# A two-layer attention encoder: value products over four query tiles, half of them between a tile's two score components

## The chip, the cores and the metric

The kernel runs on one core of a Trainium2 chip. The metric is the device time of one execution in microseconds (us); several executions are timed and their median is given. TensorE (PE) multiplies matrices; VectorE (DVE), ScalarE (ACT) and GpSimd (POOL) work element by element; SyncE (SP) issues the DMAs.

## The reference

Input is `x` (1024 rows of 1024, float32). Two layers follow, each a normalised, shifted and scaled copy of `x` (scale, shift and output gate come from a conditioning vector `c`), an attention branch times a SiLU gate, an output projection and a gated residual add; a final norm closes.

```
layer 0 (8 heads): q, k: two components of 64 per head, rotated by position; v: 128 per head
    p = softmax(q1 k1 / 8) - lam * softmax(q2 k2 / 8)      # 1024 x 1024 per head
    o = p @ v;  o = rmsnorm(o) * silu(z);  x = x + gate * (o @ w_out)
layer 1 (8 heads): low-rank q (384) and kv (256), per head k_nope, q_nope of 128, a shared rotated k_pe of 64
    p = softmax((q_nope k_nope + q_pe k_pe) / sqrt(192))
    o = p @ v;  o = o * silu(z);  x = x + gate * (o @ w_out)
```

## The kernel before

Every large product is made of three matmuls (`mm3`, lines 184 to 186): both operands are split into a high and a low part, and high by high, low by high and high by low are summed in PSUM.

**Attention.** A head has two halves of four query tiles of 128 rows; a tile is the unit of the loops in `attn0` and `attn1`. In layer 0, `q_tile` makes the scores of a tile's component 0, then those of component 1, each in a PSUM tile `s` of two banks (two such tiles are in use, so each component comes back to its own one tile later). A component's scores are four matmuls of 512 columns: two halves of the keys by two stacked parts of q. VectorE takes the row maximum (line 399), ScalarE the exponential (line 401; component 1 in place), and VectorE combines both (line 781) into `e`. In layer 1, `scores1` has ten matmuls for a tile (line 1611), one maximum and one exponential.

**Turning and values.** A finished tile `e` is turned by `transpose_p` in two groups of keys, `kh` 0 and 1: four transposes into the one PSUM bank `tr` (line 382), a copy by ScalarE into `pth`, the high part (line 384), and a subtraction by VectorE into `ptl`, the low part (line 385). `pv` multiplies the turned probabilities with the value tiles `vt`: 12 matmuls for each `kh`, in which a value block of 128 x 128 is stationary and the columns of `pth` or `ptl` move. Before, `alloc_pt` gives one set of buffers to two query tiles (256 columns), with six buffers under one tag, and `pv` runs over each pair, into the left or right half of the bank `pv`, which is closed after the second pair (`close`: `head_out` and `subln` in layer 0, line 1629 and `finish` in layer 1).

**The order around a tile.** `Tail` keeps what is left to do for the two tiles before. While tile n is made, group 1 of tile n-2 is turned, and its values taken if it ends a pair; group 0 of tile n-1 is turned. In layer 0 the order is: scores 0, `fill(0)`, group 1 of n-2, `fill(1)`, scores 1, `fill(2)`, group 0 of n-1, `fill(3)`, values `kh` 0, `fill(4)`, values `kh` 1, `fill(5)`. In layer 1 group 1 of n-2 stands inside the scores (`SPL1`), and then `fill(0)`, group 0 of n-1, `fill(1)`, values, `fill(2)`, values, `fill(3)`.

**Fills.** `fill(i)` takes steps of a stream (`Stream.step`): the projections of later heads (k, q and gate z in layer 0; k, q and every second head the rotary q in layer 1). A step is one block of 128 of the contraction for a half of the rows, three matmuls of 512 columns into a bank `acc`. In layer 0 a strip has 16 steps, the stream 22 strips (352 steps). The tuples `FILL0` (heads 0 to 6), `FILL7` (head 7, its first four tiles, after which the rest is run off) and `FILL1` give the steps for each place of each tile, and `Z_PRE` those ahead of the first head. In layer 1, heads need 16 or 10 steps by turns (`steps1`), `FILL1` has 12 for every head, and what lacks is run at the head's end. A strip's weights are split by ScalarE and GpSimd (lines 229, 230) while the strip before it runs.

**Deferred work.** The rotary part of k and q is queued in `side`; each step and each tile takes one entry (`tick`). `ROT` and `DEF` say after how many entries the swapped half is multiplied and the result stored in the stacked operands.

**Start of layer 1.** `v1_tile` makes the eight value tiles of layer 1's second half of heads; `store_v` splits each into `v_hl` and stores it to DRAM (`vS`, line 364), from which `load_v` fetches a head's value tiles (line 373). The `v_hl` of these eight use the tag of the turned probabilities, six buffers.

Instructions are dispatched to each engine in an order that a planner makes from the program, so neighbours in the program can be interleaved on TensorE; an engine then runs its queue in order.

Of the kernel before, what the change touches and what calls it, by code (L numbers as in the profile page):

```python
# [12 lines left out]
F32R = mybir.dt.float32r  # L13
# [8 lines left out]
P = 128  # L22
D = 1024
T = 1024
NT = T // P
KT = D // P
HF = 512
# [7 lines left out]
for _n, _c in _W:  # L35
    VEC[_n] = (NVEC, _c)
    NVEC += _c
DEF = 7
ROT = 3
DEF1 = 0  # L40
FILL0 = ((1, 2, 1, 1, 1, 0), (1, 1, 1, 1, 1, 1)) * 3 + ((1, 2, 1, 1, 1, 0), (1, 1, 1, 1, 1, 0))
FILL1 = ((1, 0, 1, 0), (0, 1, 0, 0)) * 4
SPL1 = 2
Z_PRE = 16
V_LATE = 6
MODS = (2, 2, 2, 2, 3, 2, 0, 0)
V1_AT = (3, 2)
# [7 lines left out]
OP1 = (12, 4)  # L55
LAST = [(((0, 1, 2, 3), 0, HF),), (((0, 1), 0, HF), ((2,), 0, HF), ((3,), 0, 256), ((3,), 256, HF))]
Z_LAST = 4
FILL7 = ((0, 1, 1, 1, 1, 0),) * 4
G_WAIT = 3
G1_AT = 7  # L60
VB = (2, 3)
# [24 lines left out]
def trunk(ctx: ExitStack, tc: tile.TileContext, A, out):  # L86
    nc = tc.nc
# [95 lines left out]
    def mm3(psum, ah, al, bh, bl, first, last):  # L183
        PE.matmul(psum, ah, bh, start=first, stop=False)  # L184
        PE.matmul(psum, ah, bl, start=False, stop=False)  # L185
        PE.matmul(psum, al, bh, start=False, stop=last)  # L186
# [94 lines left out]
    class Side:  # L281


        def __init__(self):
            self.q = []
# [70 lines left out]
            SP.dma_start(f32v(t[64:128, 0, :]), f32v(t[0:64, 0, :]))  # L356
            SP.dma_start(f32v(t[0:64, 1, :]), f32v(t[64:128, 1, :]))

    def store_v(l, sp, acc, tt, fh, tag="vst", bufs=None):
        v = sp.tile([P, 2, HF], F32R, name="v_hl", tag=tag, bufs=bufs or VB[l])  # L360
        S.copy(v[:, 0, :], acc)
        V.tensor_sub(v[:, 1, :], acc, f32v(v[:, 0, :]))  # L362
        th, tl = tt // 4, tt % 4
        SP.dma_start(
            vS[l][fh][:, th, :, :, tl, :].rearrange("h p l d -> p l h d"),
            f32v(v).rearrange("p l (h d) -> p l h d", h=4),
        )
# [19 lines left out]
    def pv(o_, vt, pth, ptl, kh):  # L387
        for j in range(4):
            mm3(o_, vt[kh][:, 0, j, :], vt[kh][:, 1, j, :], pth[kh][:, j, :], ptl[kh][:, j, :], kh + j == 0, kh * 4 + j == NT - 1)

    def alloc_pt(ap_):
        pth = [ap_.tile([P, 4, 2 * P], F32R, name="pth", tag="pt", bufs=6) for _ in range(2)]
        ptl = [ap_.tile([P, 4, 2 * P], F32R, name="ptl", tag="pt", bufs=6) for _ in range(2)]
        return pth, ptl

    def softmax_part(ap_, s_ps, zs, bufs=3):

# [471 lines left out]
    class Tail:  # L869


        def __init__(self, qp, t, e, zz, c):
            self.qp, self.t, self.e, self.zz, self.c = qp, t, e, zz, c
            self.mate = tails[1]

        def turn(self, kh):
            if kh == 0:
                self.pt = alloc_pt(self.c["pool"]) if self.t == 0 else self.mate.pt
                self.mate = None
            transpose_p(self.e, *self.pt, self.t, kh)  # L880

        def pv(self, kh):
            c, qp = self.c, self.qp
            if self.t == 0:
                return
            if kh == 0:
                if qp == 0:
                    c["vt"] = load_v(c["pool"], c["l"], c["h"])
                if qp % 2 == 0:
                    c["o_"] = bank("pv", "pv")  # L890
                    c["open"](qp // 2)
            cs = slice((qp % 2) * 256, (qp % 2) * 256 + 256)
            pv(c["o_"][:, cs], c["vt"], *self.pt, kh)
            if kh == 1 and qp % 2 == 1:
                c["close"](qp // 2, c["o_"], self.zz)

    tails, hooks = [None, None], []

    def run_tails(fill):

        prev, last = tails
        prev.turn(1)
        fill(0)
        last.turn(0)
        prev.pv(0)
        prev.pv(1)
        fill(1)
        last.turn(1)
        fill(2)
        last.pv(0)  # L910
        last.pv(1)
        tails[:] = [None, None]

    def after_scores(fill, n):

        prev, last = tails
        if last:
            last.turn(0)
        fill(n)
        if prev:  # L920
            prev.pv(0)
        fill(n + 1)
        new = hooks[:]
        if prev:
            prev.pv(1)
        fill(n + 2)
        for f in new:
            hooks.remove(f)
            f()

    def attn0(h, fills, extra=None, late=None):

        def close(half, o_, zz):
            if late and half == 1:
                ctx_["late"] = late(o_, zz)
                return
            o = a0b.tile([P, HF], F32, name="o", tag="o", bufs=2)
            sq = a0b.tile([P, HF], F32, name="osq", tag="osq", bufs=4)
            head_out(o_, o, sq)
            subln(o, sq, zz, half, h, None)  # L940

        ctx_ = dict(pool=a0b, l=0, h=h, open=lambda half: None, close=close)
        for qp in range(4):
            half = qp // 2
            if qp % 2 == 0:
                zz = first.pop(0) if first else sm.tile([P, 4], F32, name="zz")
            for t in range(2):
                fl = fills(qp * 2 + t)

                def fill(i):  # L950
                    if fl[i]:
                        stream0.step(fl[i])

                def mid(c):
                    if c == 0:
                        fill(0)
                        if tails[0]:
                            tails[0].turn(1)
                        fill(1)

                if first:
                    e0 = first.pop()
                else:
                    e0 = q_tile(h, half, (qp * 2 + t) % 4, zz, a0b, mid)
                    fill(2)
                    after_scores(fill, 3)
                side.tick()
                tails[:] = [tails[1], Tail(qp, t, e0, zz, ctx_)]
                if extra:
                    extra(qp * 2 + t)  # L970
        if late:
            run_tails(lambda i: extra(8 + i))
            while hooks:
                hooks.pop(0)()
            return ctx_["late"]
# [492 lines left out]
            G.tensor_sub(l_, raw, f32v(h_))  # L1468
            wk[k][fh] = (h_, l_)

    def v1_tile(tt, fh, sp, *buf):
# [5 lines left out]
        store_v(1, sp, acc, tt, fh, *buf)  # L1477

    CK, CQ = [[None, None] for _ in range(2)], [[None, None] for _ in range(3)]

# [61 lines left out]
    gate1 = gate_steps()  # L1542
# [75 lines left out]
    def attn1(h, fills, extra=None, late=None):  # L1618

        def open_(half):  # L1620
            ctx_["gz"] = wst.tile([P, HF], F32, name="gz1", tag="gz", bufs=3)
            SP.dma_start(ctx_["gz"], zS[h, half])

        def close(half, o_, zz):
            if late and half == 1:
                ctx_["late"] = late(o_, zz, ctx_["gz"])
                return
            o = ap2.tile([P, HF], F32, name="o1", tag="o", bufs=2)
            V.scalar_tensor_tensor(out=o, in0=o_, scalar=0.5, in1=ctx_["gz"], op0=ALU.mult, op1=ALU.mult)
            V.reciprocal(zz, zz)  # L1630
            finish(o, zz, 1, h, half, None, ap2, None)

        ctx_ = dict(pool=ap, l=1, h=h, open=open_, close=close)
        for qp in range(4):
            half = qp // 2
            if qp % 2 == 0:
                zz = first1.pop(0) if first1 else sm.tile([P, 4], F32, name="zz1")
            for t in range(2):
                ti = (qp * 2 + t) % 4
                fl = fills(qp * 2 + t)  # L1640

# [10 lines left out]
                tails[:] = [tails[1], Tail(qp, t, e, zz, ctx_)]  # L1652
                if extra:
                    extra(qp * 2 + t)
        if late:
            run_tails(lambda i: extra(8 + i))
            while hooks:
                hooks.pop(0)()
            return ctx_["late"]

    stream1.step(6)
    v1_left = list(range(NT))
    for n, steps in zip(V1_AT, (steps1[0] - 6, 0)):
        for tt in v1_left[:n]:
            v1_tile(tt, 1, ap, "pt", 6)
        del v1_left[:n]
        stream1.step(steps)
    side.flush()
# [1 line left out]
    zz0 = sm.tile([P, 4], F32, name="zz1")  # L1670
    first1 += [zz0, scores1(0, 0, 0, zz0)]
    for tt in v1_left:
        v1_tile(tt, 1, ap, "pt", 6)
    stv.close()
    ap2 = pool(st5, "attn1b")
    for h in range(NH - 1):
        attn1(h, lambda i: FILL1[i], lambda i: next(gate1, None))
        while late_q:
            late_q.pop(0)()
        stream1.step(sum(steps1[: h + 2]) - stream1.count)  # L1680
# [162 lines left out]
```

## Time and profile before

| | us |
|---|---|
| median of 3 runs | 1441.8 |
| lowest and highest | 1441.35, 1442.82 |
| the profiled execution | 1438.65 |
| its span, first to last instruction | 1436.9 |

Layer 0's attention lies between about 165 and 690 us of the span, layer 1's between about 975 and 1347. How a line of groups reads: line, engine, operation, output and inputs by name, shape, count, then busy time and mean duration of one, then the idle time of that engine just ahead of them and what ended it. A timeline row has start, duration, engine, line, operation, operands, shape and count of merged neighbours.

### The profile page before, as it was taken

How to read it: one execution, taken by the hardware profiler on the slowest of the kernel's cores; microseconds unless marked ns; L12 is line 12 of the kernel's file. 1: busy time of each engine (PE TensorE's matmuls, PEld its weight loads, DVE VectorE, ACT ScalarE, POOL GpSimd, SP SyncE). 2: the span in 40 equal slices, each digit the busy share in tenths (PEclk: the TensorE clock that was granted, in tenths of full speed). 3: DMA queues.
4: the chain of work that ended last, by engine and by line, in shares of the span. 5: the costliest groups of instructions: out<-in, count | busy, mean ns of one | idle time of the engine just before them, and what ended most of it. 6: DMA issues, size and time to landing. Idle time of an engine off the chain costs nothing. (4 is left out here: it accounts for less than half of the span.)

```text
span 1436.9 us, 20644 instructions
## 1 busy us (share of the span) xinstructions
PE 1388.8 (97%) x7388; PEld 1158.8 (81%) x7388; DVE 917.5 (64%) x1372; ACT 728.7 (51%) x1287; POOL 610.6 (42%) x483
## 2 busy tenths in 40 slices
PE   5999999999999999998999999999999999999997
PEld 4778788888888888887787877887888888888886
DVE  6656877767777767677435985545666555555355
ACT  5622375666565656566343452335455554545342
POOL 4416164656464646464461343532141331412572
PEclk9999999999999999999999999999999999999999
DMA  8787723333332333237653145398343432336563
GB/s 326 238 254 237 255 70 93 84 104 81 96 101 84 96 89 91 86 96 248 236 183 125 38 132 184 122 305 236 133 130 111 130 101 77 104 96 217 185 237 136
DMA packets 135527, 213.70 MB, mean 149 GB/s; under 512 B 19072, under 2 KB 56064, under 8 KB 135424
## 3 DMA queue, kind: packets, MB, share of 16 engines
q1 hardware_dynamic: 135424, 212.38, 47.1%
q8 instruction: 58, 0.95, 0.3%
q14 instruction: 45, 0.37, 0.1%
HBM read 137.92 MB, written 50.80 MB: 131 GB/s over the span
## 5 line engine op out<-in xcount | busy, mean ns | idle before, releaser
L384 ACT CAST pth<-tr 128x512 fp32r<-128x512 f32 x256 | 150.6, 588 | 284.2 <-PE tr L382 281.9
L399 DVE TENSOR_REDUCE nm<-s 128x1 f32<-128x1024 f32 x192 | 234.1, 1219 | 77.2 <-PE s L773 65.7
L385 DVE TENSOR_TENSOR ptl<-tr,pth 128x512 fp32r<-128x512 f32 x256 | 176.2, 688 | 139.4 <-ACT pth L384 138.9
L230 POOL TENSOR_TENSOR wl<-wraw,wh 128x512 fp32r<-128x512 f32 (+2 forms) x79 | 103.6, 1314 | 205.6 <-ACT wh L229 183.4
L401 ACT ACTIVATE e<-s,nm 128x1024 f32<-128x1024 f32 x128 | 143.7, 1123 | 29.8 <-DVE nm L399 29.2
L382 PE MATMUL tr<-ident,e 128*128 128x128 f32 x1024 | 155.1, 274 | 2.3 <-DVE ptl L385 2.0
L382 PEld LDWEIGHTS tr<-ident,e 128*128 128x128 f32 x1024 | 121.2, 140 | 43.6 <-DVE ptl L385 19.2
L184 PE MATMUL acc<-h0h,wh 128*128 128x512 f32 x360 | 150.1, 417 | 1.9 <-DVE v_hl L362 1.8
L184 PE MATMUL pv<-pth,vt 128*128 128x256 f32 x512 | 147.1, 287 | 0.0
L185 PE MATMUL pv<-ptl,vt 128*128 128x256 f32 x512 | 145.8, 285 | 0.0
L186 PE MATMUL pv<-pth,vt 128*128 128x256 f32 x512 | 144.7, 283 | 0.0
L186 PE MATMUL acc<-h0h,wl 128*128 128x512 f32 x360 | 143.1, 398 | 0.5 <-POOL wl L230 0.5
L185 PE MATMUL acc<-h0l,wh 128*128 128x512 f32 x360 | 142.0, 394 | 0.0
L1013 POOL TENSOR_TENSOR wol<-wor,woh 128x512 fp32r<-128x512 f32 x64 | 85.0, 1351 | 84.7 <-ACT woh L1012 77.2
L185 PEld LDWEIGHTS pv<-ptl,vt 128*128 128x128 f32 x512 | 97.6, 191 | 2.9
L184 PEld LDWEIGHTS pv<-pth,vt 128*128 128x128 f32 x512 | 97.4, 190 | 2.9 <-ACT pth L384 0.2
L186 PEld LDWEIGHTS pv<-pth,vt 128*128 128x128 f32 x512 | 97.6, 191 | 0.1
L326 POOL TENSOR_TENSOR rp_r<-rp_raw,cosT 128x512 f32<-128x512 f32 x38 | 49.8, 1311 | 91.0 <-ACT rp_raw L321 50.8
L331 POOL TENSOR_TENSOR rp_sw<-rp_sw,sinT 128x512 f32<-128x512 f32 x42 | 55.4, 1318 | 74.1 <-DMA rp_sw<-rp_raw 73.9
L773 PE MATMUL s<-ks,qa 128*128 128x512 f32 x256 | 82.6, 404 | 2.8 <-DVE e L781 2.6
L781 DVE SCALAR_TENSOR_TENSOR e<-s,z,e 128x1024 f32<-128x1024 f32 x64 | 82.1, 1283 | 2.1
L773 PE MATMUL s<-ks,qb 128*128 128x512 f32 x256 | 81.1, 395 | 0.0
(590 smaller groups left out, 3335.4 us busy)
## 6 DMA issues: line engine op xcount, KB each, us to landing
ada<-in_ada_ss SPq DMA_DIRECT2D x32, 512.0 KB, 6.0
wraw<-in_w_s SPq DMA_DIRECT2D x64, 256.0 KB, 2.9
vS<-v_hl SPq DMA_DIRECT2D x32, 512.0 KB, 5.9
vt<-vS SPq DMA_DIRECT2D x32, 512.0 KB, 3.7
wor<-in_w_out SPq DMA_DIRECT2D x64, 256.0 KB, 3.9
rp_sw<-rp_raw SPq DMA_DIRECT2D x168, 64.0 KB, 2.0
bc_s<-bc_d SPq DMA_DIRECT2D x34, 256.0 KB, 4.1
oS<-bc_s SPq DMA_DIRECT2D x30, 256.0 KB, 2.5
```

The source lines that it names most:

```text
L184: PE.matmul(psum, ah, bh, start=first, stop=False)
L185: PE.matmul(psum, ah, bl, start=False, stop=False)
L186: PE.matmul(psum, al, bh, start=False, stop=last)
L230: sub = (V if pair_of else G).tensor_sub(l_[:, :n], raw[:, :n], f32v(h_[:, :n]))
L382: PE.transpose(tr[:, j, :], p[:, kt * P : (kt + 1) * P], ident)
L384: mk["S"] = S.copy(pth[kh][:, :, dst], tr).ins
L385: mk["V"] = V.tensor_sub(ptl[kh][:, :, dst], tr, f32v(pth[kh][:, :, dst])).ins
L399: mk["V"] = V.reduce_max(nm, s_ps, axis=AX.X, negate=True).ins
L401: mk["S"] = S.activation(e, s_ps, AF.Exp, bias=nm, scale=1.0, accum_out=zs).ins
L773: PE.matmul(s_ps[:, kc * HF : (kc + 1) * HF], src[:, c, ql], KS[h][kc][:, c, :], start=fst, stop=not fst)
L781: combined.append(V.scalar_tensor_tensor(out=e0, in0=e1, scalar=z1[:, 0:1], in1=e0, op0=ALU.mult, op1=ALU.add).ins)
L1013: in_turn(G.tensor_sub(lo, raw, f32v(hi)))
```

## The change

- The turned probabilities of four tiles lie side by side (512 columns); `pt_tile` gives each of `pth` and `ptl` one buffer for each `kh` (two under each of two tags, that is one set).
- `pv` runs over 512 columns once in four tiles, when the half's last tile is turned. In the second half of head 7 of either layer it still runs over pairs (`pairs`).
- In layer 0 the values' `kh` 0 stands between the scores of components 0 and 1, right behind group 1 of tile n-2; in layer 1 it stands ahead of group 0 of tile n-1.
- `FILL0` has 8 steps in three tiles of four and none in the tile that takes the values; head 7 has 6 steps, `Z_PRE` is 18, and `FILL1` has the 16 or 10 steps that the next head needs. `DEF` is 9 for 7, `ROT` 4 for 3.
- The eight late value tiles of layer 1 share the new buffers, two to a buffer (`v1_home`).
- The scratch for software-made DMAs is set to 1024 bytes.

```diff
-DEF = 7
-ROT = 3
+DEF = 9
+ROT = 4
-FILL0 = ((1, 2, 1, 1, 1, 0), (1, 1, 1, 1, 1, 1)) * 3 + ((1, 2, 1, 1, 1, 0), (1, 1, 1, 1, 1, 0))
-FILL1 = ((1, 0, 1, 0), (0, 1, 0, 0)) * 4
+FILL0 = ((2, 2, 1, 2, 0, 1), (0, 0, 0, 0, 0, 0), (2, 2, 1, 2, 0, 1), (2, 2, 1, 2, 0, 1)) * 2
+FILL1 = {16: ((1, 1, 0, 1), (0, 0, 0, 0), (1, 1, 0, 1), (1, 1, 0, 0)) * 2, 10: ((1, 1, 0, 0), (0, 0, 0, 0), (1, 1, 0, 0), (1, 0, 0, 0)) * 2}
-Z_PRE = 16
+Z_PRE = 18
-FILL7 = ((0, 1, 1, 1, 1, 0),) * 4
+FILL7 = ((1, 1, 0, 1, 0, 0), (0, 0, 0, 0, 0, 0), (1, 1, 0, 0, 0, 0), (1, 0, 0, 0, 0, 0))
...
+    def pv(o_, vt, pth, ptl, kh, cs):
         for j in range(4):
+            mm3(o_[:, cs], vt[kh][:, 0, j, :], vt[kh][:, 1, j, :], pth[kh][:, j, cs], ptl[kh][:, j, cs], kh + j == 0, kh * 4 + j == NT - 1)
+
+    def pt_tile(ap_, kh, name):
+        return ap_.tile([P, 4, HF], F32R, name=name, tag=f"pt{kh}", bufs=2)
...
         def turn(self, kh):
+            if self.i == 0:
+                for parts, name in zip(self.pt, ("pth", "ptl")):
+                    parts[kh] = pt_tile(self.c["pool"], kh, name)
+            transpose_p(self.e, *self.pt, self.i, kh)
+
+        def due(self):
+            return self.i == 3 or (self.pairs and self.i == 1)
...
+            cs = slice((self.i - 1) * P, (self.i + 1) * P) if self.pairs else slice(0, HF)
+            pv(c["o_"], c["vt"], *self.pt, kh, cs)
+            if kh == 1 and self.i == 3:
+                c["close"](half, c["o_"], self.zz)
...
     def after_scores(fill, n):
         prev, last = tails
+        if prev and prev.c["l"]:
+            prev.pv(0)
         if last:
             last.turn(0)
         fill(n)
-        if prev:
-            prev.pv(0)
         fill(n + 1)
...
                         if tails[0]:
                             tails[0].turn(1)
+                            tails[0].pv(0)
                         fill(1)
...
+    def v1_home(tt):
+        if tt % 2 == 0:
+            v1_bufs.append(pt_tile(ap, (tt // 2) % 2, "v_hl"))
+        return v1_bufs[-1][:, tt % 2 * 2 : tt % 2 * 2 + 2, :]
...
-        attn1(h, lambda i: FILL1[i], lambda i: next(gate1, None))
+        attn1(h, lambda i: FILL1[steps1[h + 1]][i], lambda i: next(gate1, None))
...
+    nc = bacc.Bacc("TRN2", target_bir_lowering=False, num_devices=1, dynamic_dma_scratch_size=1024)
```

More of the change, by code (lines that the diff above doesn't have):

```diff
@@ L357, in stack_q, with store_v @@
             SP.dma_start(f32v(t[0:64, 1, :]), f32v(t[64:128, 1, :]))
-    def store_v(l, sp, acc, tt, fh, tag="vst", bufs=None):
-        v = sp.tile([P, 2, HF], F32R, name="v_hl", tag=tag, bufs=bufs or VB[l])
+    def store_v(l, sp, acc, tt, fh, tag="vst", bufs=None, v=None):
+        if v is None:
+            v = sp.tile([P, 2, HF], F32R, name="v_hl", tag=tag, bufs=bufs or VB[l])
         S.copy(v[:, 0, :], acc)
@@ L385, in transpose_p @@
         mk["V"] = V.tensor_sub(ptl[kh][:, :, dst], tr, f32v(pth[kh][:, :, dst])).ins
-    def pv(o_, vt, pth, ptl, kh):
+    def pv(o_, vt, pth, ptl, kh, cs):
         for j in range(4):
[L389 to L394, printed above, removed]
+            mm3(o_[:, cs], vt[kh][:, 0, j, :], vt[kh][:, 1, j, :], pth[kh][:, j, cs], ptl[kh][:, j, cs], kh + j == 0, kh * 4 + j == NT - 1)
+    def pt_tile(ap_, kh, name):
+        return ap_.tile([P, 4, HF], F32R, name=name, tag=f"pt{kh}", bufs=2)
     def softmax_part(ap_, s_ps, zs, bufs=3):
@@ L869, in trunk, with __init__ @@
     class Tail:
-        def __init__(self, qp, t, e, zz, c):
-            self.qp, self.t, self.e, self.zz, self.c = qp, t, e, zz, c
-            self.mate = tails[1]
-        def turn(self, kh):
[L877 to L880, printed above, removed]
+        def __init__(self, ti, e, zz, c, pairs):
+            self.ti, self.e, self.zz, self.c = ti, e, zz, c
+            self.i = ti % 4
+            self.pairs = pairs
+            if self.i == 0:
+                c["pt"] = [None, None], [None, None]
+            self.pt = c["pt"]
+        def turn(self, kh):
+            if self.i == 0:
+                for parts, name in zip(self.pt, ("pth", "ptl")):
[3 more added lines that the diff above has]
+            return self.i == 3 or (self.pairs and self.i == 1)
         def pv(self, kh):
-            c, qp = self.c, self.qp
-            if self.t == 0:
+            c, half = self.c, self.ti // 4
+            if not self.due():
                 return
             if kh == 0:
-                if qp == 0:
+                if half == 0 and "vt" not in c:
                     c["vt"] = load_v(c["pool"], c["l"], c["h"])
-                if qp % 2 == 0:
+                if self.i < 2 or not self.pairs:
                     c["o_"] = bank("pv", "pv")
[L891 to L895, printed above, removed]
+                    c["open"](half)
+            cs = slice((self.i - 1) * P, (self.i + 1) * P) if self.pairs else slice(0, HF)
+            pv(c["o_"], c["vt"], *self.pt, kh, cs)
+            if kh == 1 and self.i == 3:
+                c["close"](half, c["o_"], self.zz)
     tails, hooks = [None, None], []
@@ L904, in run_tails @@
         last.turn(0)
-        prev.pv(0)
-        prev.pv(1)
         fill(1)
@@ L967, in attn0 @@
                 side.tick()
-                tails[:] = [tails[1], Tail(qp, t, e0, zz, ctx_)]
+                tails[:] = [tails[1], Tail(qp * 2 + t, e0, zz, ctx_, bool(late) and half == 1)]
                 if extra:
@@ L1469, in load_wk, with v1_tile @@
             wk[k][fh] = (h_, l_)
-    def v1_tile(tt, fh, sp, *buf):
+    def v1_tile(tt, fh, sp, *buf, home=None):
         acc = bank("acc", "vps")
@@ L1476, in v1_tile @@
             mm3(acc, ch[:, c_], cl[:, c_], wk[k][fh][0], wk[k][fh][1], k == 0, k == 1)
-        store_v(1, sp, acc, tt, fh, *buf)
+        store_v(1, sp, acc, tt, fh, *buf, v=home)
     CK, CQ = [[None, None] for _ in range(2)], [[None, None] for _ in range(3)]
@@ L1651, in attn1 @@
                     after_scores(fill, 1)
-                tails[:] = [tails[1], Tail(qp, t, e, zz, ctx_)]
+                tails[:] = [tails[1], Tail(qp * 2 + t, e, zz, ctx_, bool(late) and half == 1)]
                 if extra:
@@ L1659, in attn1 @@
             return ctx_["late"]
+    v1_bufs = []
+    def v1_home(tt):
+        if tt % 2 == 0:
+            v1_bufs.append(pt_tile(ap, (tt // 2) % 2, "v_hl"))
+        return v1_bufs[-1][:, tt % 2 * 2 : tt % 2 * 2 + 2, :]
     stream1.step(6)
@@ L1664, in trunk @@
         for tt in v1_left[:n]:
-            v1_tile(tt, 1, ap, "pt", 6)
+            v1_tile(tt, 1, ap, home=v1_home(tt))
         del v1_left[:n]
@@ L1672, in trunk @@
     for tt in v1_left:
-        v1_tile(tt, 1, ap, "pt", 6)
+        v1_tile(tt, 1, ap, home=v1_home(tt))
     stv.close()
@@ L1830 @@
     from concourse.bass_utils import run_bass_kernel_spmd
-    nc = bacc.Bacc("TRN2", target_bir_lowering=False, num_devices=1)
+    nc = bacc.Bacc("TRN2", target_bir_lowering=False, num_devices=1, dynamic_dma_scratch_size=1024)
     A = layout(inputs)
```

1 line of the change is left out of this document (removed).

## The prediction

> **What bounds the kernel now.** I read the page first, then the busy time by stretch, then the timeline of TensorE around single tiles.
>
> ```profile
> span 1436.9 us, 20644 instructions
> PE 1388.8 (97%) x7388; PEld 1158.8 (81%) x7388; DVE 917.5 (64%) x1372; ACT 728.7 (51%) x1287; POOL 610.6 (42%) x483
> ...
> PEclk9999999999999999999999999999999999999999
> ...
> L184 PE MATMUL pv<-pth,vt 128*128 128x256 f32 x512 | 147.1, 287 | 0.0
> L185 PE MATMUL pv<-ptl,vt 128*128 128x256 f32 x512 | 145.8, 285 | 0.0
> L186 PE MATMUL pv<-pth,vt 128*128 128x256 f32 x512 | 144.7, 283 | 0.0
> ```
>
> TensorE is busy 97% of the span at a full granted clock, and the next engine 64%. There are 1536 value products of 256 columns. Their mean of about 285 ns is not their price, since neighbours overlap; the price is the distance from start to start, below. First: is TensorE gapless in both attentions?
>
> ```profile
> 165.00:231.00 66.00, 65.89 (x363) 55.34 (x364) 51.59 (x72) 42.90 (x76) 33.70 (x27) 1.00 0.35 100
> 231.00:297.00 66.00, 66.00 (x368) 56.14 (x367) 46.79 (x68) 40.75 (x72) 38.66 (x32) 1.00 0.35 96
> ...
> 563.00:628.00 65.00, 63.92 (x359) 53.48 (x358) 45.70 (x68) 40.06 (x71) 35.81 (x30) 1.00 0.32 94
> 628.00:690.00 62.00, 57.20 (x339) 47.68 (x338) 46.44 (x70) 38.72 (x68) 23.50 (x20) 1.00 0.54 183
> ```
> ```profile
> 1166.00:1211.00 45.00, 45.00 (x276) 38.68 (x275) 24.18 (x34) 22.21 (x41) 7.40 (x6) 1.00 0.29 86
> ```
>
> The columns are the stretch, its length, then busy time of TensorE, its weight loads, VectorE, ScalarE and GpSimd. A whole head of layer 0 (231 to 297) and one of layer 1 (1166 to 1211) leave TensorE no idle time. So a nanosecond saved on TensorE there counts, as long as no other engine becomes late. The exception is layer 0's head 7 (628 to 690), with 4.8 us idle.
>
> **Term 1: half as many value products, each twice as wide.** The last half of head 7 keeps pairs in either layer, 2 of 32 halves. So 1440 of the 1536 products become 720, 360 in each layer. The timeline of TensorE gives start-to-start distances, layer 0 first:
>
> ```profile
> 626.52 0.28 PE L184 MATMUL pv<-pth,vt 128*128 128x256 f32 x1
> ...
> 627.95 0.63 PE L773 MATMUL s<-ks,qa 128*128 128x512 f32 x2
> ```
> ```profile
> 404.90 0.39 PE L184 MATMUL acc<-h0h,wh 128*128 128x512 f32 x1
> ...
> 405.61 0.60 PE L382 MATMUL tr<-ident,e 128*128 128x128 f32 x4
> 405.96 0.48 PE L184 MATMUL acc<-h0h,wh 128*128 128x512 f32 x1
> 406.28 0.39 PE L185 MATMUL acc<-h0l,wh 128*128 128x512 f32 x1
> ...
> 409.07 0.60 PE L382 MATMUL tr<-ident,e 128*128 128x128 f32 x4
> ```
> ```profile
> 1160.23 0.39 PE L184 MATMUL acc<-ckh,wh 128*128 128x512 f32 x1
> ...
> 1162.98 0.60 PE L382 MATMUL tr<-ident,e 128*128 128x128 f32 x4
> ...
> 1165.03 0.61 PE L382 MATMUL tr<-ident,e 128*128 128x128 f32 x4
> ...
> 1167.56 0.60 PE L382 MATMUL tr<-ident,e 128*128 128x128 f32 x4
> ```
> ```profile
> 1170.18 0.28 PE L185 MATMUL pv<-ptl,vt 128*128 128x256 f32 x1
> ...
> 1172.94 0.63 PE L1611 MATMUL s<-kn_h,qn_h 128*128 128x512 f32 x2
> ```
>
> Layer 0: 12 value products in 1.43 us, 119.2 ns each; 12 matmuls of 512 columns from 406.28 to 409.07, 232.5 ns each. Two old ones against one new: 238.4 - 232.5 = 5.9 ns, times 360 is 2.1 us. Layer 1: 23 value products in 2.76 us, 120.0 ns; 12 of 512 columns from 1160.23 to 1162.98, 229.2 ns; 10.8 ns times 360 is 3.9 us. Sum: **-6.0 us**. Wide value products do not exist in this trace, so both ends come from other wide matmuls. The slowest run near is 404.90 to 405.61, three in 0.71 us, 236.7 ns: 360 x 1.7 + 360 x 3.3 ns = 1.8 us saved. The quickest is in the quiet stage before layer 1:
>
> ```profile
> 949.97 0.39 PE L184 MATMUL vps<-wvh,ckh 128*128 128x512 f32 x1
> ...
> 955.41 0.39 PE L184 MATMUL vps<-wvh,ckh 128*128 128x512 f32 x1
> ```
>
> 24 in 5.44 us are 226.7 ns: 360 x 11.7 + 360 x 13.3 ns = 9.0 us saved. I take the middle, because scores and strips run in the same attention, between the same copies.
>
> The Trainium skill (TensorE: Matmul & The Clock Gate, Back-to-back issue gap) gives an isolated warm matmul N / 2.4 + 2.5 ns, so joining two would save one fixed 2.5 ns. By that rule 720 joins bring 1.8 us; the rows above, with 5.9 and 10.8 ns, say more, and they decide.
>
> **Term 2: the order in layer 0.** With 232.5 ns a tile has 8 score matmuls (1.86 us), two groups of four transposes (405.61 to 406.28 less one wide matmul, 0.44 us a group) and steps of 0.70 us. Before, six steps a tile and values in every second one: 6.9 and 9.8 us by turns. After, three tiles of eight steps (1.86 + 0.88 + 5.6 = 8.3 us) and one without steps that holds 24 wide products (5.6 us, also 8.3 us). All are level. The chain that can be late is: second scores, maximum, exponential, combination, and only then the next tile's second scores into the same PSUM tile. Where TensorE is bare of other work it shows alone:
>
> ```profile
> 657.02 0.73 PE L773 MATMUL s<-ks,qa 128*128 128x512 f32 x2 [0.92 <-DVE e L781]
> ...
> 663.56 0.73 PE L773 MATMUL s<-ks,qa 128*128 128x512 f32 x2 [0.67 <-DVE e L781]
> ```
>
> It needs up to 6.54 us. After, 8.3 us lie between second scores everywhere (first half of the values ahead of them, second half behind). So the idle time of the steady heads, 0.11 + 1.08 us in the first and third stretch shown, should go: **-1.2 us**; between 0 and that. The later counts for the rotary work (9 for 7, 4 for 3) are nine ticks a tile in place of seven, about the same time; GpSimd, busy 38.66 of 66 us, gets its work in three tiles of four, some 80% there, and the strips' low parts have seven steps (7 us) before use. I cost that at nothing.
>
> Moved with the values is the load of a head's value tiles, two DMAs on SP's queue:
>
> ```profile
> vt<-vS SPq DMA_DIRECT2D x32, 512.0 KB, 3.7
> ```
>
> It stood just ahead of the first value products and does so still, two tiles later and with the tile before it as the last that issues swaps ahead of it on that queue. The value products' groups above show no idle time before them, so it costs nothing; if it came only with the products, 3.7 us a head. In layer 1 the first half of the values now stands ahead of the next tile's transposes, 2.8 us; who waits for these is the copy-out, in a tile of 8.7 us. The buffers of the probabilities are one set now. The next half's first copy into it needs the first half of the values done, which the new order puts ahead of those transposes in both layers: no wait. Counting steps per head only moves two steps from some heads' ends into tiles: the same matmuls, nothing. The smaller scratch for DMAs made by software touches nothing here, since the kernel's DMAs are on SP.
>
> **Term 3: layer 0's head 7.** The stream has 352 steps; head 7 gets 6 of them instead of 13, and from head 6 it takes 2.8 us more of value products.
>
> ```profile
> 630.00 0.63 PE L773 MATMUL s<-ks,qa 128*128 128x512 f32 x2
> ...
> 635.97 0.69 PE L773 MATMUL s<-ks,qa 128*128 128x512 f32 x2
> ...
> 670.72 0.62 PE L773 MATMUL s<-ks,qa 128*128 128x512 f32 x2
> ...
> 679.26 0.63 PE L773 MATMUL s<-ks,qa 128*128 128x512 f32 x2
> ```
>
> From tile 0's second scores to tile 7's it takes 49.3 us now. After, the work between successive second scores is 6.2, 6.9, 3.4, 2.7, 5.5, 5.5 and 5.6 us. With the chain at 6.54 us that is 6 x 6.54 + 6.9 = 46.1 us, and I leave 1.4 us of the wait for an output weight that is in the 49.3:
>
> ```profile
> 675.91 0.50 PE L185 MATMUL oacc<-wol,oth 128*128 128x512 f32 x1 [1.68 <-POOL wol L1013]
> ```
>
> So 47.5 us, 1.8 less, while 4.9 - 2.8 = 2.1 us of work went elsewhere: 0.3 us lost. At 7.16 us a tile (663.56 to the next, 670.72) it would be about 3 lost; at 5.97 us (630.00 to 635.97, a tile full of work) 3 gained. I take **+0.5 us**. Head 0's tile 1 has neither steps nor values, 2.7 us of work against 6.54; eight steps stand ready behind it. Between 0 and 3.8 us; **+0.5**.
>
> **Term 4: the start of layer 1.** The value tiles now lie in the buffers of the transposed probabilities, two to a buffer.
>
> ```profile
> 977.64 0.50 PE L184 MATMUL vps<-wvh,ckh 128*128 128x512 f32 x1 [1.32 <-DVE v_hl L362]
> ```
> ```profile
> 981.59 5.31 SPq L364 DMA_DIRECT2D vS<-v_hl  x5
> ```
>
> Before, the first two low parts took the buffers of value tiles 4 and 5; after, those of 5 and 7, whose stores leave 1.06 us (5.31 / 5) and 2.1 us later. VectorE waits for them, with the maxima of the next tiles behind it and TensorE behind these. Between -1.3 (the wait at 977.64 gone) and +3; **+1.2 us**.
>
> **Term 5: transposes in layer 1.** A tile there has 10 score matmuls (2.3 us), two groups of transposes (0.9) and steps of 0.69 us. After, the tiles without values have 3, 3, 2 steps (5.2, 5.2, 4.5 us) in heads with sixteen, 2, 2, 1 (4.5, 4.5, 3.9) in those with ten, none in head 7 (3.2 each). The one PSUM bank of the transposes must be copied out by ScalarE and VectorE between groups. How fast can it turn?
>
> ```profile
> 1299.22 0.60 PE L382 MATMUL tr<-ident,e 128*128 128x128 f32 x4
> ...
> 1301.29 0.60 PE L382 MATMUL tr<-ident,e 128*128 128x128 f32 x4
> ...
> 1303.37 0.60 PE L382 MATMUL tr<-ident,e 128*128 128x128 f32 x4
> ```
>
> 2.07 us, twice in a row, with TensorE never idle. Three tiles need 6 x 2.07 = 12.4 us; ten-step heads have 12.9. Head 7 has 9.6 and may draw on the next tile's scores, 2.3 us: 0.5 to 2.9 us late, **+0.8**.
>
> Sum: -6.0 - 1.2 + 0.5 + 0.5 + 1.2 + 0.8 = **-4.2 us**. The profiled execution took 1438.65 us, 1.75 around its span of 1436.9, so it would be 1434.5. The median of the runs is 3.15 us above it; the same difference gives **1437.6 us**. A measurement of this kernel can tell about 0.2%, 2.9 us, from no change.
>
> **The rivals.** (a) Slower: the transposes' bank becomes the bound of layer 1. It decides from a mean turn of 12.9 / 6 = 2.15 us, as three short tiles now follow each other. Between 1165.03 and 1167.56 a turn took 2.53 us; with 2.3 us, three tiles take 13.8: 0.9 us late in each of 8 places of the ten-step heads, 4.3 in head 7, 11.5 in all for the 0.8 of term 5. Then 1441.8 - 4.2 + 10.7 = **1448.3 us**. For it speaks that VectorE's and ScalarE's queues also hold the maxima, exponentials and strips in less time; against it the two turns of 2.07 us, and the scores that can run ahead. 0.22.
>
> (b) No change: wide value products run at 236.7 ns like the slowest wide ones here, saving 1.8 us, and terms 2 to 5 add up as above to +1.8: **1441.8 us**. For it speaks that the run at 404.90 stands in the attention itself, against it the longer run after it at 232.5. 0.20. The rule of the Trainium skill in term 1 gives the same 1.8 us.
>
> (c) More: wide products run at 226.7 ns, saving 9.0 us, with the other terms as they are: **1434.6 us**. The few copies beside a run of 12 speak for it, the strips' 229 to 232 ns against. 0.13.
>
> (d) The change does not do what it says: the values' first half slides behind the second scores, as the order written into the queues is not always that of the program. Then term 2's 1.2 us are lost: **1438.8 us**. 0.03.
>
> **How the numbers follow.** The forecast has 0.42. Faster by over 0.2% are it, (c) and (d), just, 0.58; within, (b), 0.20; slower, (a), 0.22. The range takes in (c) and term 3's better end down to 1433.5, and the lower part of (a), up to 1446.5.
>
> **What would show it.** The value products appear as 240 of 512 columns and 32 of 256 for each of three lines. Term 1 is right if their distance is 229 to 233 ns. Term 2: tiles of layer 0 evenly 8.3 us apart and no TensorE wait for the combination between 165 and 620 us. Terms 3 and 4: idle time of 5 us in head 7 and of up to 3 at layer 1's start. It is wrong if TensorE waits for the transposes' copies in layer 1's short tiles, or if the distance is 236 ns or more.

## The result and the profile after

The changed kernel takes **1454.74 us** in the median (1451.8 to 1459.22), beside 1441.93 of the kernel before: a ratio of **1.0091 [1.0064, 1.0118]**, 13 us slower. The profiled execution took 1459.22 us, with a span of 1457.4. The prediction said 1437.6, and its range ended at 1446.5.

The page of the changed kernel (span, busy shares, groups of the value products):

```profile
span 1457.4 us, 19199 instructions
PE 1395.2 (96%) x6668; PEld 1130.6 (78%) x6668; DVE 930.8 (64%) x1372; ACT 725.4 (50%) x1287; POOL 609.4 (42%) x483
...
L184 PE MATMUL pv<-pth,vt 128*128 128x512 f32 (+1 forms) x272 | 107.4, 395 | 1.3 <-ACT pth L385 1.3
L185 PE MATMUL pv<-ptl,vt 128*128 128x512 f32 (+1 forms) x272 | 104.4, 384 | 0.0
L186 PE MATMUL pv<-pth,vt 128*128 128x512 f32 (+1 forms) x272 | 103.2, 379 | 0.0
```

240 wide and 32 narrow products a line: the change does what it says. TensorE issues 720 matmuls less and is busy 6.4 us longer. The busy time by stretch clears the attentions:

```profile
231.00:297.00 66.00, 66.00 (x326) 54.05 (x325) 47.80 (x68) 39.91 (x72) 36.79 (x31) 1.00 0.32 93
563.00:628.00 65.00, 65.00 (x321) 53.23 (x320) 47.82 (x69) 39.38 (x71) 36.05 (x30) 1.00 0.34 97
```
```profile
1185.00:1230.00 45.00, 45.00 (x231) 36.66 (x230) 24.79 (x34) 23.24 (x45) 8.28 (x7) 1.00 0.31 94
```

No idle time is left there, and the distances in the timeline of TensorE are those of term 1:

```profile
351.05 0.39 PE L185 MATMUL pv<-ptl,vt 128*128 128x512 f32 x1
...
353.36 0.39 PE L186 MATMUL pv<-pth,vt 128*128 128x512 f32 x1
```
```profile
1190.79 0.39 PE L185 MATMUL pv<-ptl,vt 128*128 128x512 f32 x1
...
1193.06 0.40 PE L186 MATMUL pv<-pth,vt 128*128 128x512 f32 x1
```

Ten distances in 2.31 us are 231.0 ns, in layer 1 ten in 2.27 us, 227.0 ns. The loss stands ahead of all this, where layer 0's projections and the value tiles of its second half of heads (`vps`) are made. The same 44 us, of the kernel before and of the changed one; then again in that order, only what belongs to `vps`:

```profile
84.00:128.00 44.00, 41.92 (x180) 33.07 (x179) 29.05 (x42) 17.62 (x30) 18.95 (x13) 1.00 0.82 243
```
```profile
84.00:128.00 44.00, 31.08 (x119) 23.55 (x118) 31.18 (x43) 15.50 (x27) 15.38 (x11) 0.90 0.79 249
```
```profile
84.00:128.00 44.00, 16.98 (x71) 13.29 (x72) 0.69 (x1) 1.18 (x2) 1.00 0.82 243
```
```profile
84.00:128.00 44.00, 1.14 (x3) 0.83 (x3) 0.00 (x0) 0.00 (x0) 0.90 0.79 249
```

TensorE does 10.8 us less in the changed kernel. Before, 71 value matmuls stood between and behind the half products of k, q and z; now 3 do. What TensorE waits for in these 44 us, before and changed (`rp_raw` is the copy of a half product of k or q out of its bank, `gz` the gate made of one of z):

```profile
PE vps L184 <- ACT wvh L547: 0.7, 1, 0.7
PE acc L184 <- DVE v_hl L362: 0.6, 1, 0.6
PE acc L186 <- POOL wl L230: 0.5, 1, 0.5
```
```profile
PE acc L184 <- ACT rp_raw L321: 5.0, 1, 5.0
PE vps L184 <- DVE gz L711: 4.3, 1, 4.3
PE acc L184 <- ACT rp_raw L323: 1.5, 2, 1.1
PE acc L184 <- DVE v_hl L363: 1.5, 1, 1.5
PE acc L186 <- POOL wl L230: 0.7, 1, 0.7
```

The copies are little later than before (`rp_raw` 2.3 us, `gz` 3.2 us); what hid them is gone. The long waits cost more than their length, as the timeline of the changed kernel shows:

```profile
100.66 0.80 PE L184 MATMUL acc<-h0h,wq 128*128 128x512 f32 x1 [5.01 <-ACT rp_raw L321]
101.25 0.63 PE L185 MATMUL acc<-h0l,wq 128*128 128x512 f32 x1
...
104.66 0.63 PE L184 MATMUL acc<-h0h,wq 128*128 128x512 f32 x1
...
105.46 0.39 PE L186 MATMUL acc<-h0h,wq 128*128 128x512 f32 x1
```
```profile
104.00:105.00 1.00, 1.00 (x4) 0.80 (x3) 0.00 (x0) 0.00 (x0) 0.00 (x0) 0.50 0.94 339
```

Behind 5.01 us of idle time eight distances from 101.25 take 3.41 us, 426 ns each in place of 231, with the granted clock at 0.50; from 105.46 on they are 231 ns again. That is some 2 us on top of the 5.

The lengths of the stages by events in the traces (us). The events are TensorE's first score of a layer and the first reading of a finished bank `pv` by the engine that closes a half; the columns to the right are experiments below.

```
                                        before   changed  16 early  strip in  narrow    layer 0
                                        (twice)           steps     pair      products  alone
start to the first scores             153.1 155.1  180.0   153.4     155.7     156.4     155.3
to head 0's end of scores and values   79.7  81.5   71.3    78.8      79.5      80.6      78.9
to the middle of head 6               377.5 377.8  375.8   375.8     375.8     378.7     375.8
to the middle of head 7                57.8  58.1   58.8    58.9      57.9      58.1      58.0
to layer 1's first scores             306.1 306.0  307.4   306.6     306.8     303.5     305.8
to layer 1's last half                372.1 372.0  372.5   371.8     371.8     373.2     373.0
to the end                             90.5  91.5   91.6    92.0      91.3      91.1      91.3
```

The changed kernel's first two rows together are 251.3 us, before 232.8 and 236.6: 14.7 and 18.5 us lost there, and all else within 1.5 us or better than before.

### The profile page after: what moved, and what is told of

Same layout as the page of the kernel before. It is cut to its first block, busy times and chain, and to the rows that moved or that the text cites. A ratio compares the mean times of both kernels' runs of the same rounds, so it can differ in the third digit from the quotient of the medians.

```text
span 1457.4 us, 19199 instructions
## 1 busy us (share of the span) xinstructions
PE 1395.2 (96%) x6668; PEld 1130.6 (78%) x6668; DVE 930.8 (64%) x1372; ACT 725.4 (50%) x1287; POOL 609.4 (42%) x483
## 5 line engine op out<-in xcount | busy, mean ns | idle before, releaser
L184 PE MATMUL pv<-pth,vt 128*128 128x512 f32 (+1 forms) x272 | 107.4, 395 | 1.3 <-ACT pth L385 1.3
L185 PE MATMUL pv<-ptl,vt 128*128 128x512 f32 (+1 forms) x272 | 104.4, 384 | 0.0
L186 PE MATMUL pv<-pth,vt 128*128 128x512 f32 (+1 forms) x272 | 103.2, 379 | 0.0
L772 PE MATMUL s<-ks,qa 128*128 128x512 f32 x256 | 85.8, 408 | 4.9 <-DVE e L780 3.7
L186 PEld LDWEIGHTS acc<-h0h,wl 128*128 128x128 f32 x360 | 67.8, 188 | 17.1 <-POOL wl L230 2.1
L184 PEld LDWEIGHTS acc<-h0h,wh 128*128 128x128 f32 x360 | 68.2, 189 | 15.9 <-ACT rp_raw L323 2.3
L185 PEld LDWEIGHTS acc<-h0l,wh 128*128 128x128 f32 x360 | 68.5, 190 | 12.2
L810 POOL TENSOR_TENSOR o<-o,bc_s 128x512 f32<-128x512 f32 x30 | 46.4, 1546 | 71.6 <-DVE o L1634 63.0
```

Of the source, the lines that this page charges most:

```text
L772: PE.matmul(s_ps[:, kc * HF : (kc + 1) * HF], src[:, c, ql], KS[h][kc][:, c, :], start=fst, stop=not fst)
```

## The experiments

The line of the diff that acts there is `Z_PRE`, 18 for 16: two steps of a further strip (k of head 1) now stand in the program ahead of the value tiles. The stream's first strip is the gate z of head 0; k of head 1 is its second, so its first half is the third half to be opened, and "third strip" below means that half. A strip half takes a PSUM bank with its first step. The banks `acc` come by turns from a set of two and a set of three: the gate strip's two halves took the two, value tiles 0 to 2 the three. With a third strip ahead, that one takes the first of the three. (The diffs below are shortened, with remarks added.)

**Back to 16, and the steps elsewhere.** First theory: value tile 0 loses the bank that came free early.

```diff
-Z_PRE = 18
+Z_PRE = 16
+ attn0: head 0, tile 1 takes (1, 1, 0, 0, 0, 0)
```

> The changed kernel with the count of early strip steps back at 16; its two steps go into tile 1 of head 0, all else as changed. Theory (bank): with 18 steps a third PSUM bank is opened for a strip ahead of the value tiles, takes the place that value tile 0 had, and TensorE loses the value products it worked off between the half products of k, q and z. Then this kernel has those products back, the first row of scores starts near 153 us as before the change (180 with it), the first combination of head 0 is closed near 199 us and not 218, and the time falls by 15 to 19 us, to 1436 to 1440. Rival (buffers or the smaller scratch for DMAs): the value stores and their waits are late because the memory is laid out otherwise; nothing of that is undone, and the time stays at 1452 to 1459. Rival (work): the two steps alone are moved, 1.4 us of TensorE either way, so 1452 to 1458.

1439.81 us, ratio **0.9973 [0.9959, 0.9987]**; in the 44 us:

```profile
84.00:128.00 44.00, 41.77 (x178) 32.90 (x178) 30.00 (x43) 17.58 (x31) 19.23 (x13) 1.00 0.84 245
```

All is back with one constant, its two steps now in head 0's tile 1: 0.0118 or 17 us by the two ratios (69 records of `vps` in the 44 us). The changed buffers and the smaller scratch are still in this kernel, so they have no part in the loss.

**The same two steps, behind value tile 1.**

```diff
-Z_PRE = 18
+Z_PRE = 16
         v0_tile(tt, 1, wv1)
+        if tt == 1:
+            stream0.step(2)
```

> The changed kernel with 16 early steps and the other two issued behind value tile 1 of layer 0, so still ahead of the attention. All 18 steps are done as early as in the changed kernel, but value tiles 0 and 1 take their banks before the third strip does. Theory (bank): near the kernel with 16, 1436 to 1442 us. Rival (it is the early place of two more steps, with their weights and their spills, that costs): like the changed kernel, 1452 to 1459.

0.9991 [0.9978, 1.0005], 1441.8 us. The steps still stand ahead of the attention and cost little: their order against the value tiles matters.

**The kernel before with 18 steps, and with 17.**

```diff
-Z_PRE = 16
+Z_PRE = 18      # second kernel: 17
```

> The kernel before with 18 early steps in place of 16 and nothing else. Theory (bank): the value products lose their place between the half products here too, and the time rises by 12 to 19 us, to 1454 to 1461. Rival (buffers or scratch of the change): those are not here, so at most the two steps' own 1.4 us, 1440 to 1444.

> The kernel before with 17 early steps. The seventeenth is the one that opens the third strip's bank. Theory (bank): a jump, the whole loss of the kernel with 18 at once, 1453 to 1461. Rival (each early step costs its share): half the loss of the kernel with 18, 1448 to 1451.

1.0108 [1.0084, 1.0132] and 1.0089 [1.0061, 1.0117]. The old kernel with this one constant loses as much as the whole change, and three matmuls are nearly as bad as six: a jump, not a price per step. With 18 steps it keeps as few value products in the 44 us as the changed kernel:

```profile
84.00:128.00 44.00, 1.65 (x3) 1.16 (x4) 0.00 (x0) 0.00 (x0) 0.87 0.80 247
```

**Value tile 0's bank taken first; the steps behind value tile 0.** Is it the bank, or the place in the program?

```diff
+    stream0.step(16)
+    acc0 = bank("acc", "vps")     # used by v0_tile(0)
+    stream0.step(2)
```
```diff
-Z_PRE = 18
+Z_PRE = 16
+        if tt == 0:
+            stream0.step(2)       # behind v0_tile(0)
```

> The changed kernel with its 18 early steps, and the PSUM bank of value tile 0 taken between step 16 and step 17, so that value tile 0 has the bank that it had before the change and the third strip has the next one; the matmuls stand in the program in the same order as in the changed kernel. Theory A (who owns the bank that is free early): value tile 0 can be worked off early again, 24 of its products come back as filler, and the time falls to 1438 to 1448. Theory B (place in the queue: whatever the program has behind a strip that has no bank yet is not pulled ahead of it, even with a bank of its own): nothing comes back, 1452 to 1459.

> The changed kernel with 16 early steps and the other two behind value tile 0. Theory B: only the value tile ahead of the third strip, 24 matmuls of 0.23 us, 5.5 us of work, fills TensorE's waits there, where it was 60 with both steps in head 0 and 47 with them behind tile 1; the time lies between, 5 to 9 us under the changed kernel: 1446 to 1450. Theory A: as with tiles 0 and 1 ahead, 1440 to 1443.

1.0109 [1.0090, 1.0128] and 1.0062 [1.0040, 1.0084]. The first theory fell: with the bank reserved nothing came back. The second kernel, at 1450.76 us, comes out just above the range that its 24 matmuls gave it (1446 to 1450). `vps` in the 44 us with the steps behind tile 1, behind tile 0, and with the bank first:

```profile
84.00:128.00 44.00, 14.44 (x55) 10.58 (x55) 0.69 (x1) 0.59 (x1) 0.96 0.82 248
```
```profile
84.00:128.00 44.00, 7.61 (x27) 5.25 (x27) 0.68 (x1) 0.59 (x1) 0.96 0.85 255
```
```profile
84.00:128.00 44.00, 0.63 (x2) 0.59 (x3) 0.00 (x0) 0.00 (x0) 0.92 0.83 258
```

With the kernel before that makes 71, 55, 27 and 2 matmul records beside ratios of 1, 0.9991, 1.0062 and 1.0109. The first of these still has its narrow products; the like case is the changed kernel with 16 steps, 69 records and 0.9973.

**Fewer early steps.**

```diff
-Z_PRE = 16
+Z_PRE = 8       # head 0's tile 1 takes (2, 2, 2, 2, 1, 1)
```

> The changed kernel with 8 early steps; the next ten stand in tile 1 of head 0, which has 2.7 us of other work against a chain of 6.5. One strip half is opened ahead of the value tiles in place of two (three in the changed kernel). If fewer early strips only help as far as TensorE still waits there: the waits left between 84 and 126 us are 2.8 us and in head 0's first tiles 3.3, so 1 to 4 us under the kernel with 16, 1436 to 1439. If the ten steps in tile 1 overfill it, or the gate strip comes late for the first half's end: the same or up to 3 us more, 1440 to 1443.

1.0060 [1.0044, 1.0076], 1450.65 us: a miss. TensorE waits for an exponential:

```profile
151.94 1.22 PE L772 MATMUL s<-ks,qa 128*128 128x512 f32 x2 [7.70 <-ACT e L400]
```

The first scores came 11 us earlier, and with more value products (82) spent before 128 us none ran beside them. It seems that the filler is worth something only where it lies; the ten steps in tile 1 were moved by the same edit, and no run tells the two apart.

**The set of banks.** All 18 steps in place, the third strip's bank from the set of two; and 16 steps with the gate strip's banks from the set of three, that of the value tiles.

```diff
+    stream0.step(16)
+    turn = 0                     # the third strip: a bank of the two
+    stream0.step(2)
+    turn = 2                     # value tiles 0 to 2: the three, as before
```
```diff
+    turn = 2                     # the gate strip: banks of the three
     stream0.step(16)
```

> The changed kernel with all its 18 early steps in their place ahead of the value tiles; only the third strip takes its PSUM bank from the set of two in place of the set of three, from which value tiles 0 to 2 take theirs. Theory B as it stands (nothing behind a strip that waits is pulled ahead): the filler stays away, 1452 to 1459 us. Theory C (TensorE's groups that take a bank of the same set keep their order, those of another set may be passed): the value products are back between the half products, about 70 before 128 us, and the time is that of the kernel with 16 early steps, 1437 to 1441.

> The changed kernel with 16 early steps, and the two halves of the gate strip, which stand ahead of the value tiles, take their banks from the set of three. No third strip is opened early. Theory C: value tile 0 stands behind them in that set, the filler is lost as with 18 steps: 1450 to 1457 us. Theory that it is the third strip's steps ahead of the value tiles (B): as with 16 steps, 1437 to 1441.

1.0004 [0.9992, 1.0016] and 1.0011 [0.9996, 1.0025]. First kernel, all of the stretch and `vps` alone:

```profile
84.00:128.00 44.00, 42.07 (x181) 33.20 (x180) 30.89 (x45) 18.05 (x31) 17.13 (x12) 1.00 0.83 249
```
```profile
84.00:128.00 44.00, 15.28 (x62) 11.56 (x62) 0.69 (x1) 0.59 (x1) 1.00 0.83 249
```

With the steps in their place and only the set changed, the value products are back and 0.0087 of the ratio, 12.5 us, with them. So the set decides, and not the place alone. The second kernel lost part of it: 40 records, all of them behind the gate strip and none between the half products, and one of the two long waits is back.

```profile
84.00:128.00 44.00, 8.99 (x40) 7.66 (x41) 0.00 (x0) 0.00 (x0) 0.96 0.83 252
```
```profile
PE acc L184 <- ACT rp_raw L321: 3.9, 1, 3.9
```

Its 1.0011 is 5.5 us above the kernel with 16 steps, by ratios taken on two chips, short of the 10 or more that theory C wanted, and not the nothing of theory B. The value products come in one run behind the half products, while in the changed kernel the third strip's six matmuls stand behind the first three of them and take 3.4 us; the wait for `gz` does not return. That the planner lets a group wait behind an earlier one of its set fits all these orders; the planner's rule itself no run shows.

**The kernel before again.** No edit.

> The kernel before once more, for a second profile of it. The first one was of an execution 3 us under the median; if stage by stage the two agree to 0.3 us, sections of the other kernels can be compared with it directly; if this one is longer by 2 to 4 us spread over all stages, differences of that size between profiles are not the change's.

Its span is 1441.9, 5.0 more. 3.8 us of that lie in the first two rows of the table and 1.0 in the last; each of the other four agrees to 0.35 us. Between runs of one kernel, differences of a few tenths in those rows can be read; in the first two and the last, nothing under 4 us. A shift of the strips moves them more: the kernel before with 18 and 17 early steps, nothing else changed, has 375.8 and 375.4 us to the middle of head 6, and 305.0 and 308.0 to layer 1's first scores.

**Narrow products in the new order.**

```diff
-            pv(c["o_"], c["vt"], *self.pt, kh, cs)
+            for k in range(2):      # except where pairs stay
+                pv(c["o_"], c["vt"], *self.pt, k, slice(kh * 256, kh * 256 + 256))
```

> The changed kernel with 16 early steps, and each place that has 12 products of 512 columns given 24 of 256 in their stead (the first two tiles' columns, then the other two's). Order of the parts, steps and buffers as in the kernel with 16. Theory: the cadence alone is worth the 6.0 us of term 1, so 1445 to 1447. Rival (a fixed cost of 2.5 ns a product, 1.8 us in all): 1441 to 1442. Rival (the gain is in the order and not in the width): 1439 to 1440.

1.0010 [0.9993, 1.0027], 1443.11 us, by the ratios 5.3 us above the kernel with 16 steps, with some 3 us of doubt as the two ran on different chips. Its time lies in none of the three ranges; the difference lies nearest to the first theory. The table is sharper: 378.7 for 375.8 and 373.2 for 371.8, 4.3 us in these two rows, where the two kernels differ in nothing but the width. The width is worth this there; the new order with narrow products is not faster than the kernel before. The row to layer 1's first scores, which has no wide product in either, is 3.1 us shorter in this kernel, and no run shows why.

**Layer 0's part alone.** Layer 1 as before: pairs, buffers, order and `FILL1`.

```diff
-Tail(qp * 2 + t, e, zz, ctx_, bool(late) and half == 1)
+Tail1(qp, t, e, zz, ctx_)        # the class before, in layer 1
```

> The changed kernel with 16 early steps, and layer 1 as before the change: value products of 256 columns behind each pair of tiles, its buffers, its order and its steps per tile. Prediction's terms for layer 1: -3.9 for the cadence, +1.2 for the start, +0.8 for the transposes, so without them 1.9 us more, 1441.7. Theory from the profile (layer 1 gains 4 us by the cadence and gives them back in idle time and in longer scores): the same time within 1 us, 1439 to 1441. Rival (the width is worth more than the profile says): 1443 or more.

0.9985 [0.9970, 1.0000], 1440.14 us, within the doubt of the kernel with 16 steps. In layer 1's row it has 373.0 for 371.8, but the kernel before, with the same code there, 372.1. TensorE's waits around the start of layer 1 (first heads; the wide kernel with 16 steps, then the kernel before again):

```profile
PE vps L184 <- DVE v_hl L363: 1.3, 1, 1.3
PE tr L383 <- DVE ptl L386: 1.0, 3, 0.5
PE pv L184 <- ACT pth L385: 0.7, 1, 0.7
PE acc L186 <- POOL wl L230: 0.6, 2, 0.3
```
```profile
PE vps L184 <- DVE v_hl L362: 1.3, 1, 1.3
PE tr L382 <- DVE ptl L385: 0.7, 1, 0.7
```

**More steps in head 7.**

```diff
-FILL0, last tile: (2, 2, 1, 2, 0, 1);  FILL7, tiles 2, 3: (1, 1, 0, 0, 0, 0), (1, 0, 0, 0, 0, 0)
+FILL0, last tile: (2, 2, 1, 2, 0, 0);  FILL7, tiles 2, 3: (1, 1, 1, 1, 0, 1), (1, 1, 1, 1, 0, 1)
```

> The changed kernel with 16 early steps, and one strip step less in the last tile of each of heads 0 to 6 of layer 0, so that head 7 has 13 steps as before the change, five each in its tiles 2 and 3. Theory: heads 0 to 6 are full of TensorE work, head 7 is bound by the chain of maxima, exponentials and the combination and shows some 6 us without work from 645 to 657 us, so 7 steps of 0.69 us, 4.9 us, go where TensorE stands idle: 3 to 5 us below the kernel with 16 early steps, 1435 to 1437. Rival: head 7 is full too, or its chain grows by the steps' own spills; then no change, 1439 to 1441.

1.0010 [0.9996, 1.0024], 1443.99 us: a miss. Its waits from 232 to 615 us, where for the kernel with 16 steps none is listed:

```profile
PE tr L383 <- DVE ptl L386: 2.0, 2, 1.4
PE s L772 <- DMA qa<-qa: 1.6, 3, 0.7
PE s L772 <- DMA qb<-qb: 0.8, 1, 0.8
```

One step less per head brings the strips' ends, and with them the swaps of q, up to their deadlines. And head 7's chain kept its idle time (8.0 us for 8.5 up to its middle) with 4.2 us of steps on top. The idle time was not where the steps went.

## Why the prediction was wrong, point by point

**The step that failed is one that it does not have.** It went through the diff edit by edit, costed steps "per head" at nothing as "the same matmuls", and has no word on `Z_PRE`: the sum puts the two steps that this constant moves ahead of the value tiles at nothing, without a reason. The work is indeed the same, 1.4 us; what it displaced cost 12.5 to 17 us (1.0091 against 1.0004 and 0.9973). The prediction asked how full TensorE is only from 165 us on. Ahead of that TensorE was full because 71 matmuls of the value tiles lay in its waits. A term for the two steps would have had to ask what lies in those waits and whether it stays there.

**Term 1 (-6.0).** The cadence was right: 231.0 and 227.0 ns, where it took 232.5 and 229.2. Distances summed over all value products, waits taken out, are 94.7 and 94.3 us in the two layers for the narrow ones, 91.6 and 90.7 for the wide ones in the same order, 6.7 us less. The rule of the Trainium skill (TensorE: Matmul & The Clock Gate, Back-to-back issue gap) gave 1.8 us; the runs speak against it. Of the 6.7 us, the lengths of the two attention rows show 4.3; the rest is outside these rows or comes back as idle time.

**Term 2 (-1.2).** The idle time went, as said: the two stretches shown have none, and of the waits from 231 to 628 us the kernel before has this one and the changed kernel none.

```profile
PE s L773 <- DVE e L781: 0.9, 1, 0.9
```

The row to the middle of head 6, which also has part of term 1, is 1.7 to 2.0 us shorter with 15 strip matmuls (3.5 us) more in it. That it is shorter does not prove the order, as the kernel before with 17 and 18 early steps is as short there; it has the 15 matmuls less. Second scores stand 8.2 to 8.3 us apart in three tiles of four and 9.4 in the fourth, so not evenly. No wait for the rotary work or the value loads shows there, as said.

**Term 3 (+1.0).** The size is about right for head 7: 57.9 to 58.9 in the row against 57.8 and 58.1. Its parts are not: from tile 0's second scores to tile 7's it takes 49.6 us with 16 early steps and 48.7 with the strip in the pair, where the term had 47.5. Head 0's tile 1 can't be told from the spread of its row.

**Term 4 (+1.2).** Its wait did not grow: 1.3 us before and after. Two waits for `wl`, 0.6 us, came, at 997 and 1029 us.

**Term 5 (+0.8).** Waits for the transposes' copies come, but in the kernel with 16 steps only from 1050 to 1072 us, in head 1 and as head 2 begins, not in every short tile and not in head 7. Layer 1's idle time on TensorE (what a distance that is over 100 ns beyond its group's median has beyond it), from its first scores to its last values, is 5.7 us for 2.9 and 2.8: +2.9 for terms 4 and 5, where they had 2.0. So layer 1 gains 0.2 to 0.4 us in its row and not 1.9.

**The sum without the early steps.** It was -4.2. The kernel with 16 steps gives -3.9 us [-5.9, -1.9] by its ratio, the one with the strip in the pair +0.6 [-1.2, +2.3]; the three attention rows that can be read (to the middle of head 6, of head 7, and layer 1's) add up to 807.4 and 807.9 us before, and to 806.5 and 805.5 in these two: 0.9 to 2.4 us shorter. But the kernel before with 18 and 17 early steps has 806.5 and 805.9 there, so these lengths do not tell the change from a shift of the strips. Shown are the cadence of term 1 and what the width is worth, 4.3 us in two rows; what the rest of the sum comes to stays open, and that -3.9 lies so near to -4.2 is in part luck.

**The rivals.** Neither (a), (b) nor (c) is what happened, and (d) did not occur. All four moved the price of what the change is about; none asked what a constant at the edge of the diff moves in a stage that the change does not touch.

By its own comparison the kernel with 16 early steps is below the kernel before (0.9973), and by the ratios below the changed one; it is the version to keep.

## What to carry to other kernels

Read every constant of a diff as a change of the instruction order, also in stages that the change is not about, and look there for work that lies in another engine's waits: the profile shows it as a full engine, and its price only when it is gone. Where banks come by turns from several sets, one more group ahead shifts every later one; count the turns, and see from which set each group takes its bank. When one part of a change is in doubt, put that constant into the old kernel: a single run shows the whole loss.

## What the runs showed of the hardware

Behind a wait of 5.01 us TensorE's granted clock stood at 0.50 for over 4 us (426 ns for 231). The Trainium skill (TensorE: Matmul & The Clock Gate, What's actually happening) has it so behind an idle window of about 3.4 us, and this row agrees. The wait need not be that long, though: in the second profile of the kernel before, behind one of 1.84 us that ends at 162.33, seven distances from 163.13 us take 2.99 us, 427 ns each. Counted over the profiles, matmuls of 512 columns at 405 to 450 ns cost 3.0 us in the first profile of the kernel before, 7.2 in its second, 12.3 in the changed kernel. So matmuls at half clock account for 4.2 of the 5.0 us between two executions of the same kernel, and for 5 to 9 us of the changed kernel's longer span, beside the waits themselves.
